# Channel mixers of a two-layer trunk: high and low part of the moving operand in one 512-column product

## The chip, the core and the metric

The kernel runs on one core of a Trainium2 chip. The metric is the device time of one execution in microseconds (us); lower is better. The engines are named as in the profile: PE multiplies matrices (PEld is its weight load), DVE and ACT are the vector and the scalar engine, POOL and SP mostly issue transfers. Results of PE land in PSUM, which the kernel uses as eight banks of 128 x 512 float32; everything else lies in SBUF. In the profile a tile carries the tag of its pool: `pmm`, `psc` and `ptr` are PSUM banks, `u`, `f`, `t`, `pt`, `wr`, `wh`, `wl` are SBUF buffers.

## The reference

The program is an encoder trunk of two layers on 512 tokens of width 1024, float32 in and out. Each layer has a token mixer (matrix memory or band attention, plus attention to 256 memory tokens), an output projection, and a channel mixer. The channel mixer is what the change is about:

```python
def conv_ffn(h, w_up, conv_w, conv_b, w_down):
    u, g = jnp.split(h @ w_up, 2, axis=-1)
    g = causal_dwconv(g, conv_w, conv_b)
    return (jax.nn.silu(g) * u) @ w_down
```

`h` is 512 x 1024 and normalised, the up projection has 2 x 2816 columns (22 tiles of 128 for `u`, 22 for the gate `g`), the convolution has width 3 along the tokens, and the sum of the result and the residual goes on to the next layer.

## The kernel before, in words

**Two parts of every number.** Operands of PE have the type float32r, so each is split into a high part and a low part: `split` (L130 to L133) makes the high part by a cast on ACT (L132) and the low part by a subtraction on DVE (L133). A product of two operands is then three products: high x high (L171), high x low (L172), low x high (L173), all in `mm3`, added up in one PSUM bank.

**Block sums.** In a channel mixer tiles 0 to 4 of the up projection are computed plainly. For tiles 5 to 21 the method `step` computes the tile of `u` and the tile of the gate together as a 2 x 2 block product, with seven chains of products in place of eight. The tokens are two halves of 256 columns (`H`), the 1024 input features two halves of four tiles. The sums of input blocks are made once (`forms`), the sums of weight blocks per step (class `Forms`). The seven chains, in the order in which PE runs them: `a11`, `a12`, `s2`, then a piece of the down projection (`down_products(0)`), `s1`, `s3`, a second piece (`down_products(1)`), `a22`, `s4`. Each chain is four calls of `mm3` with 256 columns, 12 products; a piece of the down projection is 12 products of 512 columns. Steps 9 to 20 have both pieces, steps 5 to 8 only the second, step 21 none (`UNITS`).

**Three banks a step.** `a11`, `s2`, `s3` and `a22` add up in the same bank `r1`, and after each of the four ACT copies the bank's state out (L808, L814, L824, L831): the running sum is itself wanted. `a12` goes to `r2` and is added by DVE (L811). `s1` and `s4` add up in `r3`, read by DVE after each (L825, L907).

**The order is written out.** Inside `later` the orders of PE, ACT and DVE are those of the program text (`manual_schedule`), and each engine takes its list strictly in turn. One pass of `step(j)` also does the rest of tile j-1 (class `Tail`: last block, three taps of the convolution, silu, gating, split) and makes the weights of tile j+1 (class `Forms`: sums and splits). So a step's list on DVE and ACT mixes work for three tiles, and an instruction that waits holds up all that is behind it.

**Around it.** Outside the mixers the order is left to a scheduler. Tiles `u` come from one pool of 57 buffers of 512 columns. Before each mixer `reload_x` brings the residual back from memory in eight transfers of 256 KB that SP issues (L412).

Of the kernel before, what the change touches and what calls it, by code (L numbers as in the profile page):

```python
# [16 lines left out]
P = 128  # L17
D = 1024
S = 512
# [25 lines left out]
UNITS.update((j, (2 * j - 10, 2 * j - 9)) for j in range(9, 21))  # L45
H = S // 2
# [7 lines left out]
def trunk(  # L54
# [25 lines left out]
    bufs = {"wr": 3, "wh": 3, "wl": 3, "u": 57, "t": 8, "pt": 2, "s": 16, "rb": 3, "bias": 2}  # L80
# [4 lines left out]
    def sb(tag, shape, dtype=F32):  # L85
        count[0] += 1
        return pool.tile(shape, dtype, tag=tag, name=f"{tag}{count[0]}", bufs=bufs[tag])

# [207 lines left out]
    def scaled(t, g):  # L296
        hi, lo = sb("u", [P, S], F32R), sb("u", [P, S], F32R)
# [98 lines left out]
    def x_scaled(j):  # L396
# [6 lines left out]
        acts.append((sb("u", [P, S], F32R), sb("u", [P, S], F32R)))  # L403
# [5 lines left out]
    def reload_x():  # L409
        for j in range(KT):  # L410
            xT[j] = sb("u", [P, S])
            tc.keep_in_program_order(nc.sync.dma_start(xT[j], xspill[j]))  # L412
# [6 lines left out]
    with tc.manual_schedule(engines={mybir.EngineType.PE, mybir.EngineType.Activation, mybir.EngineType.DVE}):  # L419
# [9 lines left out]
        for q in range(KT // 2 + 1):  # L429
            if q < KT // 2:  # L430
# [6 lines left out]
                hi, lo = sb("u", [P, S], F32R), sb("u", [P, S], F32R)  # L437
# [3 lines left out]
                kws.append([sb("u", [P, S], F32R).rearrange("p (a b) -> p a b", a=2) for _ in range(2)])  # L441
# [6 lines left out]
        for u in range(4):  # L448
            vws.append([sb("u", [P, S], F32R).rearrange("p (a b) -> p a b", a=2) for _ in range(2)])
# [43 lines left out]
    def head_queries(t, scale=1.0):  # L493
        qs, ls = ([sb("u", [P, S], F32R) for _ in range(2)] for _ in range(2))
# [36 lines left out]
    def values(outs):  # L531
# [5 lines left out]
        hi, lo = sb("u", [P, S], F32R), sb("u", [P, S], F32R)  # L537
# [3 lines left out]
    def queries(o, row):  # L541

        if row is None:
            return head_queries(o, HD**-0.5)
        q = sb("t", [P, S])
        V.scalar_tensor_tensor(q, o, HD**-0.5, row, op0=ALU.mult, op1=ALU.mult)
        return head_queries(q)
# [6 lines left out]
    def memory_attention(q, kv, hp, mixes):  # L554
# [46 lines left out]
        mixes[6 + hp] = values(outs)  # L601
# [34 lines left out]
    class ChannelMixer:  # L636
# [64 lines left out]
        def forms(self):  # L701

            for j in range(KT):
# [3 lines left out]
                hi, lo = sb("u", [P, S], F32R), sb("u", [P, S], F32R)  # L707
# [4 lines left out]
            for k in range(KT // 2):  # L712
# [10 lines left out]
                for t in (ta, tb):  # L723
                    hi, lo = sb("u", [P, S], F32R), sb("u", [P, S], F32R)
                    split(hi, lo, t)
                    pairs.append((hi, lo))
# [49 lines left out]
        def later(self):  # L776
# [17 lines left out]
            for part in (tail.last_block, tail.first_tap, tail.second_tap, tail.third_tap, tail.gated, tail.split):  # L794
                part()

        def step(self, j, w, nxt, tail):
# [4 lines left out]
            new = Tail(self, j)  # L802
# [8 lines left out]
            V.tensor_tensor(out=new.up[:, :H], in0=new.up[:, :H], in1=r2[:, :H], op=ALU.add)  # L811
            then(tail, "third_tap")
            self.products(r1, w.s2, self.t(2))
            A.copy(new.up[:, H:], r1[:, :H])  # L814
# [8 lines left out]
            self.products(r1, w.s3, self.t(3))  # L823
            A.copy(new.u3[:, :H], r1[:, :H])  # L824
# [5 lines left out]
            self.products(r1, w.a22, self.t(4))  # L830
            A.copy(new.pre[:, :H], r1[:, :H])  # L831
            then(nxt, "split_down", "split_gate")
            self.products(new.r3, w.s4, self.b(1, 1))
# [65 lines left out]
    class Tail:  # L899


        def __init__(self, mixer, j):
            self.mixer, self.j = mixer, j

        def last_block(self):
            c = self.up[:, H:]
            V.tensor_tensor(out=c, in0=c, in1=self.r3[:, :H], op=ALU.add)  # L907
# [592 lines left out]
```

## Time and profile before

| | us |
|---|---|
| median of the 3 runs | 1203.18 (1202.53 to 1204.07) |
| the profiled execution | 1203.12 |
| its span | 1201.4 |
| PE busy | 1191.2 (99%) |
| DVE busy | 945.9 (79%) |
| ACT busy | 708.5 (59%) |
| stretch of the first mixer's steps in the span | about 343 to 600 |
| stretch of the second mixer's steps | about 907 to 1165 |

The span is the profiled execution from its first to its last instruction; 1.7 us lie around it. Rows of a timeline give start, duration, engine, line, operation, output and inputs, and in square brackets the idle time of the engine just before and whose end it waited for. Neighbouring instructions of an engine overlap a little, so the distance from one start to the next is shorter than a duration; both are used below, and the text says which.

### The profile page before, as it was taken

What the parts mean: (1) busy time and instruction counts of PE and PEld (TensorE: products, weight loads), DVE (VectorE), ACT (ScalarE), POOL (GpSimd) and SP (SyncE); (2) the same over time, 40 slices, a digit from 0 to 9 for tenths busy, and PEclk for the clock granted to TensorE, in tenths of its full rate; (3) what the DMA queues carried; (4) which work ended last, traced back from release to release, by engine and by line L of the source; (5) the groups of instructions that cost most, each with busy time, mean ns of one, the idle gap of its engine ahead of it and who ended that gap; (6) DMA issues with size and microseconds to landing.
All of it is one profiled execution on the core that took longest, in us unless ns stands there. A gap on an engine that the chain in (4) does not pass through costs nothing.

```text
span 1201.4 us, 18749 instructions
## 1 busy us (share of the span) xinstructions
PE 1191.2 (99%) x7047; PEld 1056.8 (88%) x7047; DVE 945.9 (79%) x1722; ACT 708.5 (59%) x1260; POOL 123.4 (10%) x207
## 2 busy tenths in 40 slices
PE   9999999999999999999999999999999999999997
PEld 8988888888899999999888888888889999999986
DVE  6777687888978777777698888997897877777755
ACT  5546577644556555555565667775465655555545
POOL 2200101010021111111020000001001011011100
PEclk9999999999999999999999999999999999999999
DMA  8634221444275676665563323146336466666551
GB/s 294 203 88 123 54 53 57 152 142 123 79 176 153 154 164 155 156 142 127 141 197 110 90 71 101 51 130 204 112 97 140 111 143 133 142 141 137 120 156 70
DMA packets 199021, 156.00 MB, mean 130 GB/s; under 512 B 7865, under 2 KB 179347, under 8 KB 198931
## 3 DMA queue, kind: packets, MB, share of 16 engines
q1 hardware_dynamic: 183762, 119.73, 34.0%
q0 software_dynamic: 14592, 34.03, 14.4%
q8 instruction: 55, 0.90, 0.3%
q10 hardware_dynamic: 576, 1.05, 0.2%
q14 instruction: 36, 0.29, 0.1%
HBM read 126.27 MB, written 32.44 MB: 132 GB/s over the span
## 4 chain that ended last, share of the span: by engine, by line
PE 93%; ACT 3%; DVE 2%; DMA 0%; issue 0%; SPq 0%; DVEq 0%; ACTq 0%
PE pmm L171 18%; PE pmm L173 18%; PE pmm L172 18%; PE ptr L171 6%; PE ptr L172 6%; PE ptr L173 6%; PE psc L171 5%; PE psc L172 5%; PE psc L173 5%; PE psc L516 2%; PE ptr L1327 1%; PE ptr L1348 1%; PE ptr L1349 1%; DMA u<-in_mem_dram 0%; ACT wh L132 0%
## 5 line engine op out<-in xcount | busy, mean ns | idle before, releaser
L171 PE MATMUL pmm<-u,wh 128*128 128x512 f32 (+1 forms) x968 | 336.6, 348 | 0.1
L173 PE MATMUL pmm<-u,wl 128*128 128x512 f32 (+1 forms) x968 | 333.7, 345 | 0.0
L172 PE MATMUL pmm<-u,wh 128*128 128x512 f32 (+1 forms) x968 | 333.3, 345 | 0.1
L133 DVE TENSOR_TENSOR wl<-wr,wh 128x1024 fp32r<-128x1024 f32 (+3 forms) x172 | 199.7, 1162 | 102.4 <-ACT wh L132 101.8
L132 ACT CAST wh<-wr 128x1024 fp32r<-128x1024 f32 (+3 forms) x172 | 171.8, 1001 | 108.3 <-PE pmm L172 42.8
L173 PEld LDWEIGHTS pmm<-u,wl 128*128 128x128 f32 x968 | 183.6, 190 | 21.1
L172 PEld LDWEIGHTS pmm<-u,wh 128*128 128x128 f32 x968 | 183.8, 190 | 18.3 <-DVE u L133 0.8
L171 PEld LDWEIGHTS pmm<-u,wh 128*128 128x128 f32 x968 | 183.7, 190 | 18.0 <-ACT u L132 0.5
L171 PE MATMUL ptr<-u,wh 128*128 128x512 f32 x272 | 106.7, 392 | 0.0
L172 PE MATMUL ptr<-u,wh 128*128 128x512 f32 x272 | 106.5, 392 | 0.0
L173 PE MATMUL ptr<-u,wl 128*128 128x512 f32 x272 | 105.8, 389 | 0.0
L748 POOL DMA_DIRECT2D xspill<-t x64 | 55.5, 867 | 465.4 <-ACT t L747 454.9
L173 PE MATMUL pmm<-u,u 128*128 128x256 f32 x296 | 84.0, 284 | 0.4 <-DVE u L133 0.4
L171 PE MATMUL pmm<-u,u 128*128 128x256 f32 x296 | 84.0, 284 | 0.0
L172 PE MATMUL pmm<-u,u 128*128 128x256 f32 x296 | 83.7, 283 | 0.0
L133 DVE TENSOR_TENSOR u<-pt,u 128x512 fp32r<-128x512 f32 x102 | 70.2, 688 | 11.7 <-ACT u L132 9.1
L171 PE MATMUL psc<-u,wh 128*128 128x256 f32 (+1 forms) x232 | 76.1, 328 | 0.0
L173 PE MATMUL psc<-u,wl 128*128 128x256 f32 (+1 forms) x232 | 75.9, 327 | 0.0
L172 PE MATMUL psc<-u,wh 128*128 128x256 f32 (+1 forms) x232 | 75.9, 327 | 0.0
L747 ACT COPY t<-ptr 128x512 f32<-128x512 f32 x64 | 37.4, 585 | 60.5 <-PE ptr L173 60.5
L132 ACT CAST u<-pt 128x512 fp32r<-128x512 f32 x102 | 63.0, 617 | 11.3 <-DVE pt L857 11.3
L919 ACT ACTIVATE t<-t 128x512 f32<-128x512 f32 x34 | 21.6, 634 | 79.6 <-DVE t L656 79.6
(291 smaller groups left out, 2527.4 us busy)
## 6 DMA issues: line engine op xcount, KB each, us to landing
wr<-in_ffn_w_up_dram SPq DMA_DIRECT2D x54, 512.0 KB, 4.9
wr<-in_ffn_w_down_dram SPq DMA_DIRECT2D x38, 512.0 KB, 3.9
pt<-in_ffn_w_up_dram SPq DMA_DIRECT2D x34, 512.0 KB, 6.3
xspill<-t POOLq DMA_DIRECT2D x64, 256.0 KB, 4.8
wr<-in_a_w_in_dram SPq DMA_DIRECT2D x20, 512.0 KB, 3.9
xspill<-u POOLq DMA_DIRECT2D x32, 256.0 KB, 2.8
u<-xspill SPq DMA_DIRECT2D x32, 256.0 KB, 5.1
wr<-in_w_kv_dram SPq DMA_DIRECT2D x12, 512.0 KB, 4.0
```

What stands on the lines that cost most here:

```text
L132: high = A.copy(hi, src) if on_act else V.tensor_copy(hi, src)
L133: low = V.tensor_tensor(out=lo, in0=src, in1=f(hi), op=ALU.subtract)
L171: nc.tensor.matmul(o, lh, rh, start=first, stop=False, skip_group_check=more)
L172: nc.tensor.matmul(o, lh, rl, start=False, stop=False, skip_group_check=more)
L173: nc.tensor.matmul(o, ll, rh, start=False, stop=last, skip_group_check=more)
L516: nc.tensor.matmul(o, a, b, start=first and i == 0, stop=i == 1)
L747: A.copy(t, o)
L748: G.dma_start(xspill[j], t, accum_op=ALU.add)
L919: A.activation(self.acc, self.acc, AF.Silu)
L1327: nc.tensor.transpose(tp[:, b * P : (b + 1) * P], es[T, h][:, b * P : (b + 1) * P], ident)
L1348: nc.tensor.matmul(o2[:, s * P :], w, hi_at(pts[h], s, s, TT - s), start=s == 0, stop=False)
L1349: nc.tensor.matmul(o2[:, s * P :], w, lo_at(pts[h], s, s, TT - s), start=False, stop=s == TT - 1)
```

## The change

**Products.** In steps 9 to 20 (`WIDE`) six of the seven chains, all but `s1`, no longer use `mm3`. For each input tile there are two products in place of three: the low part of the weight with the high part of the input (256 columns), and the high part of the weight with both parts of the input at once, 512 columns: the high part's 256 and the low part's 256. The second product fills both halves of the bank, so the bank's right half holds the sum of the products with the low part.

**Additions.** The two halves of the bank have to be added. Where ACT copied the left half, DVE now adds the right half to that copy (`plus`, after `a11`, `s2`, `s3`, `a22`); `a12` gets a second addition on DVE; `s4`'s right half is added by `rest_of_block` in the next step. That is six additions of 128 x 256 a step on DVE.

**Order.** The split of the fourth weight sum (`split_fourth`) moves from the front of the step to behind the copy of `a11`, in all steps from 5 on.

**Buffers.** So that one product can read both parts, they must lie at a fixed distance: tiles' high and low part are now one buffer of 1024 columns (`duo`, tag `f`, 16 of them); the pool `u` has 25 buffers instead of 57. The same memory in all, but in two pools.

**Reload.** In the two token mixers `reload_x` stands later in the text, and POOL issues its eight transfers instead of SP.

```diff
+WIDE = range(9, 21)
-    bufs = {"wr": 3, "wh": 3, "wl": 3, "u": 57, "t": 8, "pt": 2, "s": 16, "rb": 3, "bias": 2}
+    bufs = {"wr": 3, "wh": 3, "wl": 3, "u": 25, "f": 16, "t": 8, "pt": 2, "s": 16, "rb": 3, "bias": 2}
+    def duo():
+        t = sb("f", [P, 2 * S], F32R)
+        return t[:, :S], t[:, S:]
...
-        def products(self, o, w, act, first=False):
+        def products(self, o, w, act, first=False, wide=False):
             n = KT // 2
-            for k in range(n):
-                mm3(o[:, :H], w[0][:, k], w[1][:, k], *act[k], first and k == 0, k == n - 1, True)
+            for k, (hi, lo) in enumerate(act):
+                start, stop = first and k == 0, k == n - 1
+                if wide:
+                    nc.tensor.matmul(o[:, :H], w[1][:, k], hi, start=start, stop=False, skip_group_check=True)
+                    both = bass.AP(
+                        tensor=hi.tensor, offset=hi.offset, ap=[list(hi.ap[0]), [lo.offset - hi.offset, 2], [1, H]]
+                    )
+                    nc.tensor.matmul(
+                        o.rearrange("p (a b) -> p a b", a=2), w[0][:, k], both, start=False, stop=stop,
+                        skip_group_check=True,
+                    )
+                else:
+                    mm3(o[:, :H], w[0][:, k], w[1][:, k], hi, lo, start, stop, True)
...
         def step(self, j, w, nxt, tail):
...
+            wide = j in WIDE
+            def onto_first(w, act, o, first=False):
+                self.products(r1, w, act, first, wide)
+                A.copy(o, r1[:, :H])
+                if wide:
+                    plus(o, r1[:, H:])
+            def plus(o, p):
+                V.tensor_tensor(out=o, in0=o, in1=p, op=ALU.add)
             then(tail, "last_block", "first_tap")
-            w.split_fourth()
             r1, r2, new.r3 = ps("mm"), ps("mm"), ps("sc")
             new.up, new.u3, new.pre = sb("t", [P, S]), sb("t", [P, S]), sb("t", [P, S])
-            self.products(r1, w.a11, self.b(0, 0), True)
-            A.copy(new.up[:, :H], r1[:, :H])
+            onto_first(w.a11, self.b(0, 0), new.up[:, :H], True)
+            then(tail, "rest_of_block")
+            w.split_fourth()
             then(tail, "second_tap")
-            self.products(r2, w.a12, self.b(1, 0), True)
-            V.tensor_tensor(out=new.up[:, :H], in0=new.up[:, :H], in1=r2[:, :H], op=ALU.add)
+            self.products(r2, w.a12, self.b(1, 0), True, wide)
+            plus(new.up[:, :H], r2[:, :H])
+            if wide:
+                plus(new.up[:, :H], r2[:, H:])
             then(tail, "third_tap")
-            self.products(r1, w.s2, self.t(2))
-            A.copy(new.up[:, H:], r1[:, :H])
+            onto_first(w.s2, self.t(2), new.up[:, H:])
...
-            self.products(r1, w.s3, self.t(3))
-            A.copy(new.u3[:, :H], r1[:, :H])
+            onto_first(w.s3, self.t(3), new.u3[:, :H])
...
-            self.products(r1, w.a22, self.t(4))
-            A.copy(new.pre[:, :H], r1[:, :H])
+            onto_first(w.a22, self.t(4), new.pre[:, :H])
             then(nxt, "split_down", "split_gate")
-            self.products(new.r3, w.s4, self.b(1, 1))
+            self.products(new.r3, w.s4, self.b(1, 1), False, wide)
...
-    reload_x()
     fill = chain(outp.part(0, 0, 1), outp.part(0, 2, 6), outp.part(0, 3))
...
     weave(islice(job, 13), fill, 0.85)
+    reload_x(G)
```

**What moves on DVE, front of a step.** DVE's list before, in a late step of the second mixer, from the last block of the tile before (L907) to the second sum of weight blocks (the second L857). `psc` is `r3`, `pmm` is `r2`, L656 are the taps, L133 the low part of the fourth sum.

```order
L907 TENSOR_TENSOR t2276_11722<-t2276_11722,psc2275_11721 128x256
L133 TENSOR_TENSOR u2299_11888<-pt1888_9422,u2298_11887 128x512
L656 SCALAR_TENSOR_TENSOR t2297_11885<-t2278_11724,cols2_793,t2297_11885 128x511
L811 TENSOR_TENSOR t2303_11894<-t2303_11894,pmm2301_11892 128x256
L656 SCALAR_TENSOR_TENSOR t2297_11885<-t2278_11724,cols2_793,t2297_11885 128x510
L857 TENSOR_TENSOR pt1888_9422<-pt1887_9421 128x512
L857 TENSOR_TENSOR pt1888_9422<-pt1888_9422,wr2295_11880 128x512
```

The same piece after the change; L939 is now the last block, L833 is `plus`, L143 the low part, L666 the taps, L889 the sums of weight blocks; `pmm2247` is `r1`, `pmm2248` is `r2`.

```order
L939 TENSOR_TENSOR t2224_11561<-t2224_11561,psc2223_11560 128x256
L833 TENSOR_TENSOR t2250_11713<-t2250_11713,pmm2247_11710 128x256
L939 TENSOR_TENSOR t2224_11561<-t2224_11561,psc2223_11560 128x256
L143 TENSOR_TENSOR u2254_11728<-pt1792_9110,u2253_11727 128x512
L666 SCALAR_TENSOR_TENSOR t2246_11708<-t2226_11563,cols2_769,t2246_11708 128x511
L833 TENSOR_TENSOR t2250_11713<-t2250_11713,pmm2248_11711 128x256 x2
L666 SCALAR_TENSOR_TENSOR t2246_11708<-t2226_11563,cols2_769,t2246_11708 128x510
L833 TENSOR_TENSOR t2250_11713<-t2250_11713,pmm2247_11710 128x256
L889 TENSOR_TENSOR pt1792_9110<-pt1791_9109 128x512
L889 TENSOR_TENSOR pt1792_9110<-pt1792_9110,wr2245_11705 128x512
```

Four instructions came in, and the last of them (`plus` on `s2`) now stands between the third tap and the sums of weight blocks.

**What moves on ACT, front of a step.** ACT's list before: first tap (L663), cast of the fourth sum (L132), copy of `a11` (L808), silu (L919), copy of `s2` (L814).

```order
L663 ACTIVATE t2243_11541<-t2224_11380,cols2_793 128x512
L132 CAST u2244_11543<-pt1888_9422 128x512
L808 COPY t2249_11550<-pmm2246_11547 128x256
L919 ACTIVATE t2243_11541<-t2243_11541 128x512
L814 COPY t2249_11550<-pmm2246_11547 128x256
```

After, with the new line numbers (L828 is every copy of `r1`, L955 the silu):

```order
L673 ACTIVATE t2139_11094<-t2118_10947,cols2_769 128x512
L828 COPY t2143_11099<-pmm2140_11096 128x256
L142 CAST u2146_11113<-pt1792_9110 128x512
L955 ACTIVATE t2139_11094<-t2139_11094 128x512
L828 COPY t2143_11099<-pmm2140_11096 128x256
```

The cast and the copy of `a11` change places; the copy of `s2` still stands behind the silu, which needs the third tap from DVE.

**What moves on DVE, end of a step.** Before, from the low part of the up weights (the first L133, 1024 columns) to the fourth sum:

```order
L133 TENSOR_TENSOR wl2313_11980<-wr2295_11880,wh2312_11979 128x1024
L825 TENSOR_TENSOR t2305_11896<-t2304_11895,psc2302_11893 128x256
L133 TENSOR_TENSOR wl2315_11998<-pt1888_9422,wh2314_11997 128x1024
L857 TENSOR_TENSOR pt1888_9422<-wr2295_11880,pt1888_9422 128x512
L133 TENSOR_TENSOR wl2319_12032<-wr2296_11882,wh2318_12031 128x1024
```

After, in the step whose banks are `pmm2221` (`r1`) and `psc2223` (`r3`):

```order
L143 TENSOR_TENSOR wl2236_11643<-wr2218_11551,wh2235_11642 128x1024
L833 TENSOR_TENSOR t2225_11562<-t2225_11562,pmm2221_11558 128x256
L858 TENSOR_TENSOR t2226_11563<-t2225_11562,psc2223_11560 128x256
L143 TENSOR_TENSOR wl2238_11658<-pt1792_9110,wh2237_11657 128x1024
L889 TENSOR_TENSOR pt1792_9110<-wr2218_11551,pt1792_9110 128x512
L833 TENSOR_TENSOR t2226_11563<-t2226_11563,pmm2221_11558 128x256
L143 TENSOR_TENSOR wl2242_11689<-wr2219_11553,wh2241_11688 128x1024
```

The addition for `s3` (the first L833) stands directly behind the low part of the up weights, and the one for `a22` (the second) between the fourth sum and the low part of the down weights.

More of the change, by code (lines that the diff above doesn't have):

```diff
@@ L448, in trunk @@
         for u in range(4):
-            vws.append([sb("u", [P, S], F32R).rearrange("p (a b) -> p a b", a=2) for _ in range(2)])
+            vws.append([t.rearrange("p (a b) -> p a b", a=2) for t in duo()])
             split(*vws[u], vraw[u])
@@ L489, in trunk, with head_queries @@
         keep(1, 1, vo, A.copy)
-    def head_queries(t, scale=1.0):
-        qs, ls = ([sb("u", [P, S], F32R) for _ in range(2)] for _ in range(2))
+    def head_queries(t, scale=1.0, room=None):
+        qs, ls = ((room or two)() for _ in range(2))
         for h, r in enumerate(HEADS):
@@ L723, in forms @@
                 for t in (ta, tb):
-                    hi, lo = sb("u", [P, S], F32R), sb("u", [P, S], F32R)
-                    split(hi, lo, t)
-                    pairs.append((hi, lo))
+                    pairs.append(duo())
+                    split(*pairs[-1], t)
                 self.sums.append(pairs)
@@ L1117, in a_memory_queries @@
     def a_memory_queries(hp):
-        memq[hp] = queries((yield from project(w_in, 4 * AW + 2 * AH + hp * P, act)), None)
+        memq[hp] = queries((yield from project(w_in, 4 * AW + 2 * AH + hp * P, act)), None, duo if hp else two)
     def mlstm_head(h):
@@ L1350, in band_attention @@
             yield
-        mixes[j] = values(outs)
+        mixes[j] = values(outs, two if j < 5 else duo)
     def b_memory_queries(hp):
-        memq[hp] = queries((yield from project(b_w_in, AW + hp * P, act)), norm.row)
+        memq[hp] = queries((yield from project(b_w_in, AW + hp * P, act)), norm.row, duo if hp else two)
     qkv = {}
```

59 lines of the change are left out of this document (32 added, 27 removed).

## The prediction

> **What bounds the kernel now.** I read the page first, then the busy time by stage, then the timelines of PE, DVE and ACT in one late step of a mixer. The page:
>
> ```profile
> span 1201.4 us, 18749 instructions
> PE 1191.2 (99%) x7047; PEld 1056.8 (88%) x7047; DVE 945.9 (79%) x1722; ACT 708.5 (59%) x1260; POOL 123.4 (10%) x207
> ```
>
> PE has work in 99% of the span, so time can only be won by shortening what PE does, and anything that makes PE wait is paid in full. The stage of the first mixer's steps, by engine:
>
> ```profile
> 340.00:600.00 260.00, 259.90 (x1815) 243.43 (x1814) 193.86 (x284) 145.86 (x249) 41.03 (x55) 1.00 0.64 152
> ```
>
> PE is busy for 259.90 of 260 us at full clock (1.00); DVE, the third figure, for 193.86, which is three quarters. What one product costs there is its distance to the next, in PE's timeline (40 distances in the first pair of rows, 24 in the second):
>
> ```profile
> 899.65 0.39 PE L172 MATMUL ptr<-u,wh 128*128 128x512 f32 x1
> ...
> 908.72 0.39 PE L173 MATMUL ptr<-u,wl 128*128 128x512 f32 x1
> 908.94 0.28 PE L171 MATMUL pmm<-u,wh 128*128 128x256 f32 x1
> ...
> 911.82 0.28 PE L171 MATMUL pmm<-u,u 128*128 128x256 f32 x1
> ```
>
> A product of 512 columns takes 9.07 / 40 = 0.2268 us, one of 256 takes 2.88 / 24 = 0.1200. So two of 256 cost 0.240 and one of 512 costs 0.2268: 0.0133 us are saved for each pair that is merged.
>
> The other two engines, in the step whose last block is added at 1102.11. DVE:
>
> ```profile
> 1102.11 0.41 DVE L907 TENSOR_TENSOR t<-t,psc 128x256 f32<-128x256 f32 x1
> 1102.44 0.69 DVE L133 TENSOR_TENSOR u<-pt,u 128x512 fp32r<-128x512 f32 x1
> 1103.04 0.75 DVE L656 SCALAR_TENSOR_TENSOR t<-t,cols,t 128x511 f32<-128x511 f32 x1
> 1103.71 0.42 DVE L811 TENSOR_TENSOR t<-t,pmm 128x256 f32<-128x256 f32 x1
> 1104.04 0.75 DVE L656 SCALAR_TENSOR_TENSOR t<-t,cols,t 128x510 f32<-128x510 f32 x1
> 1104.70 0.69 DVE L857 TENSOR_TENSOR pt<-pt 128x512 f32<-128x512 f32 x1
> 1105.42 0.69 DVE L857 TENSOR_TENSOR pt<-pt,wr 128x512 f32<-128x512 f32 x1
> ...
> 1108.66 0.69 DVE L133 TENSOR_TENSOR u<-t,u 128x512 fp32r<-128x512 f32 x1 [0.56 <-ACT u L132]
> 1109.61 1.23 DVE L133 TENSOR_TENSOR wl<-wr,wh 128x1024 fp32r<-128x1024 f32 x1 [0.26 <-ACT wh L132]
> ...
> 1115.93 1.23 DVE L133 TENSOR_TENSOR wl<-wr,wh 128x1024 fp32r<-128x1024 f32 x1 [2.35 <-ACT wh L132]
> 1117.07 0.69 DVE L133 TENSOR_TENSOR u<-pt,u 128x512 fp32r<-128x512 f32 x1
> 1117.67 0.41 DVE L907 TENSOR_TENSOR t<-t,psc 128x256 f32<-128x256 f32 x1
> ```
>
> and ACT:
>
> ```profile
> 1104.88 0.63 ACT L919 ACTIVATE t<-t 128x512 f32<-128x512 f32 x1 [2.53 <-DVE t L656]
> 1105.41 0.36 ACT L814 COPY t<-pmm 128x256 f32<-128x256 f32 x1
> 1106.15 0.62 ACT L132 CAST u<-pt 128x512 fp32r<-128x512 f32 x1 [0.38 <-DVE pt L857]
> 1107.52 0.59 ACT L747 COPY t<-ptr 128x512 f32<-128x512 f32 x1 [0.75 <-PE ptr L173]
> 1108.01 0.62 ACT L132 CAST u<-t 128x512 fp32r<-128x512 f32 x1
> 1108.53 1.05 ACT L132 CAST wh<-wr 128x1024 fp32r<-128x1024 f32 x1
> ...
> 1114.58 0.37 ACT L831 COPY t<-pmm 128x256 f32<-128x256 f32 x1 [0.85 <-PE pmm L173]
> 1114.85 1.05 ACT L132 CAST wh<-wr 128x1024 fp32r<-128x1024 f32 x1
> ```
>
> From L907 to the next L907 a step takes 15.56 us, which is PE's own: 7 chains x 12 x 0.120 and 24 products of 0.2268 are 15.52. The brackets are where DVE and ACT ran ahead and waited; DVE had 0.56 + 0.26 + 2.35 us to spare.
>
> **The products.** A step of the wide kind has 6 chains x 4 = 24 merged pairs, so PE's own time falls by 24 x 0.0133 = 0.32, to 15.24. With 12 such steps in two mixers that is 576 pairs and 7.7 us, the whole of what the change can win. No row before shows a product that reads its 512 columns as two runs of 256. Bounds: 0.2268 as one run, 0.240 if it behaved as two; I take 0.2268, since the runs are long and no row speaks against it.
>
> The Trainium skill ("TensorE: Matmul & The Clock Gate", Back-to-back issue gap) puts a product at its columns over 2.4 GHz plus 2.5 ns, so a merged pair would save only 2.5 ns, 1.4 us in all. The rows above show 13.3 ns, and they decide; by the page's figure PE's own step would be 15.50 and my total 0.5 higher.
>
> **The additions.** Six a step, each of the form of L811 (one operand in PSUM): 0.33 from start to start (1103.71 to 1104.04), 2.0 in all. That fits into DVE's 3.2 to spare. What matters is where they stand, since DVE and ACT take their lists in turn, and the bank `r1` may not be written before its copy and, now, its addition are done. I walked the new order with the distances above. The place that decides is the third tap: DVE's next instruction is now the addition for `s2`. It waits for ACT's copy of `s2`, which stands behind the silu, which waits for that very tap. Before, DVE went on with the sums of weight blocks. All that follows on DVE comes later by this wait, down to the addition for `s3`, and `a22` on PE waits for that one. What such a wait costs PE is seen once before, in step 21:
>
> ```profile
> 590.33 0.37 ACT L824 COPY t<-pmm 128x256 f32<-128x256 f32 x1
> 590.75 0.19 PEld L171 LDWEIGHTS pmm<-u,u 128*128 128x128 f32 x1 [0.35 <-ACT t L824]
> 590.98 0.28 PE L172 MATMUL pmm<-u,u 128*128 128x256 f32 x1
> ```
>
> The copy ends at 590.70, the load starts 0.05 later, and the second product comes at 590.98 instead of 0.12 after the load: 0.16 from the end of the copy to a product on time.
>
> So there is a closed circle, and its length is the shortest step that DVE, ACT and PE together allow. From the addition for `s3`: addition and release of PE 0.42 + 0.16; `a22` 4 x (0.120 + 0.227) less one distance, plus the last product's 0.39, 1.55, and 0.04 to ACT; copy to the low part of the down weights 1.35 (1114.58 to 1115.93); that low part 1.14, the gate's 0.60, last block 0.33; addition for `a11` 0.33, rest of the block 0.33; the fourth's low part 0.60; second tap 0.67; first addition for `a12` 0.42 + 0.03 (the second needs its result, as 1104.70 to 1105.42 is 0.72 for 0.69), the second 0.33; third tap 0.75 and 0.09 to the silu; silu 0.53; copy 0.37 + 0.03; addition for `s2` 0.33; first sum 0.72; second 0.73 to ACT's cast (1105.42 to 1106.15); cast 0.52, copy of the down piece 0.49, cast of the tile's result 0.52; cast of the up weights 1.05 + 0.03; its low part 1.14. The sum is 15.59.
>
> 15.59 is above PE's 15.24, and even above today's 15.56. So the win of a wide step is used up: `a22` waits 0.35 in each. Only step 9, which has no wide step before it, keeps its 0.32. Steps 10 to 20 are 11 x 0.03 = 0.33 longer in each mixer.
>
> **The moved split.** In steps 6, 7, 8 and 21, which stay narrow, the cast of the fourth sum now stands behind the copy of `a11`, and DVE's list waits for it. From the start of `a11`: its result at 1.60, copy 1.64, cast 1.91, low part from 2.56, second tap 3.16, addition 3.83, third tap 4.16, silu 5.00, copy of `s2` 5.53, release of PE 5.53 + 0.37 + 0.16 = 6.06. PE is through with `a11`, `a12`, `s2` and `s1` at 4 x 1.44 = 5.76. `s3` waits 0.30, 4 times a mixer: 1.2.
>
> **Buffers and reload.** In the token mixers PE is as full, so these can only cost. The two pools hold as many columns as one held, and the tiles of `duo` are freed together. I price both at nothing, with 1.5 us either way for a scheduler's other order. The reload moves off SP to POOL, behind the last mask of the last head:
>
> ```profile
> xspill<-t POOLq DMA_DIRECT2D x64, 256.0 KB, 4.8
> 237.59 0.64 POOL L1135 TENSOR_SCALAR_AFFINE_SELECT t<-t 128x128 f32<-128x128 f32 x1 [0.52 <-ACT t L1133]
> ...
> 257.38 0.69 DVE L629 TENSOR_TENSOR u<-u,pmm 128x512 f32<-128x512 f32 x1 [1.02 <-PE pmm L173]
> ```
>
> Between the end of that mask and the first use lie 19 us, and such a transfer takes 4.8 to land: hidden.
>
> **Sum.** Per mixer -0.32 + 0.33 + 1.2 = 1.2, for two 2.4. On the profiled execution's 1203.12 (0.06 from the median) that is 1205.5.
>
> **Rivals.** (1) *The cover holds*: the circle is shorter than 15.24 and PE runs through. For it speaks DVE's idle share; against it that 0.35 would have to be wrong in a sum whose terms are rows of the same step. Then 1203.1 - 7.7 + 2.4 = 1197.8. This is the other side, and it decides at a circle of 15.24.
> (2) *Dearer waits*: the silu's release took 0.09 where others took 0.03. If the three new ones in the circle (copy to addition, addition to addition, addition to PE) each cost 0.06 more, it is 15.77, 22 x 0.18 = 4.0 more: 1209.5.
> (3) *Late reload*: if POOL's eight transfers land 2 us after the first use in both layers, 1209.5; the 19 us speak against it.
> (4) *The change doesn't do what it says*: a product in two runs takes 0.240. PE's own time stays, `a22` in the circle is 0.05 longer, so 1.1 more: 1206.6.
>
> The Trainium skill ("Perfetto Trace Analysis", Optimizing Tensor Performance, Matmuls) advises both larger products and a change of banks between chains, so that reading one out overlaps the next. This change takes the first and makes the second worse. In the trace before, the reuse of `r1` stopped PE in step 21 (0.35, above); by the first advice alone it would be rival 1.
>
> **Chances.** The forecast 0.63, rival 1 0.11, rival 2 0.16, rivals 3 and 4 0.05 each. A measurement of this kernel can tell about 0.2%, 2.4 us, from no change, and the forecast lies on that bound. Of its 0.63 I put 0.22 above 1205.6, 0.38 within, and 0.03 below 1200.8. With the rivals: faster 0.14, same 0.40 (0.02 from rival 4), slower 0.46. The range: down, 0.1 of error in the circle is 2.2, and 1.5 for the order elsewhere, with something over for rival 1; up, rival 2 with half a microsecond over: 1199.5 to 1210. Rival 1 itself is left out.
>
> **What would show it.** Right: products of 512 columns at 0.227 in the mixers; a wait of about 0.35 a step on PE before `a22`, on DVE; about 1 us of idle DVE before the addition for `s2`, on ACT's copy; steps of 15.6 us; 0.3 before `s3` in steps 6 to 8. Wrong: steps of 15.24 with no such waits (rival 1), steps over 15.7, or PE idle for microseconds outside the mixers.

## The result and the profile after

| | before | after |
|---|---|---|
| median us (runs) | 1203.62 (4 runs, 1202.53 to 1205.06) | 1211.99 (4 runs, 1211.44 to 1212.88) |
| span of the profiled execution, us | 1201.4 | 1211.1 |
| wide step of a mixer (10 to 20), us | 15.56 | 15.60 to 15.62 |

Steps 9 to 20, where the change merges products, are called wide here, the others (5 to 8 and 21) narrow. The changed kernel is slower by 0.7%: 1.0069 of the time before, with a 95% interval of 1.0057 to 1.0081, or 8.4 us. The forecast was 1205.5, its range ended at 1210.0. The page of the kernel after:

```profile
span 1211.1 us, 17719 instructions
PE 1196.9 (99%) x6471; PEld 1024.7 (85%) x6471; DVE 995.5 (82%) x1866; ACT 707.3 (58%) x1260; POOL 131.5 (11%) x223
```

576 products are gone, and yet PE is busy for 5.7 us more: part of what it waits is counted as busy (the row at 489.48 below is a product of 256 columns that takes 0.39). So the page's busy time says nothing here; what tells is where PE falls behind. For that each product of the profile after was set beside the same product of the profile before; the lag is how much later it starts. It grows by these amounts, and by nothing in the stretches not listed:

| stage (us of before) | lag grows by |
|---|---|
| start, 0 to 31 | 0.9 |
| first token mixer, 31 to 319 | 0.3 |
| plain tiles before the first mixer, 319 to 334 | 1.3 |
| first mixer, 349 to 612 | 1.5 |
| 612 to 778 | -0.5 |
| second token mixer, 778 to 838 | 3.0 |
| plain tiles before the second mixer, 884 to 899 | 1.4 |
| second mixer, 914 to 1161 | 1.7 |

The 0.9 at the start is a tile that landed later in this one execution (mixers as before, copy before silu and fourth split in front, which have the same start, lag by 0.1 at most). The two mixers lose 3.2. Three short stretches outside them lose 5.7, and of these the prediction said that they cost nothing.

**The mixers.** The stretch from 340 to 600 by engine, and what PE's weight loads wait for in it (total, times, longest):

```profile
340.00:600.00 260.00, 259.82 (x1523) 226.71 (x1522) 219.28 (x356) 145.07 (x249) 41.69 (x56) 1.00 0.67 148
```

```profile
PEld pmm L777 <- DVE t L833: 4.5, 11, 0.5
PEld pmm L181 <- ACT t L828: 1.3, 5, 0.3
```

DVE went from 193.86 to 219.28 us, still 84%: it is not the bound by its sum. L833 is the new addition, L828 the copy ahead of it. There are eleven waits for the addition, one in each wide step from 10 on, 0.41 each; of the five for the copy, four are those of the narrow steps, 0.23 each, and one stood before too. DVE and ACT around the addition for `s2` and the one for `s3` show why:

```profile
481.71 0.74 DVE L666 SCALAR_TENSOR_TENSOR t<-t,cols,t 128x510 f32<-128x510 f32 x1
483.48 0.42 DVE L833 TENSOR_TENSOR t<-t,pmm 128x256 f32<-128x256 f32 x1 [1.02 <-ACT t L828]
...
489.01 0.41 DVE L833 TENSOR_TENSOR t<-t,pmm 128x256 f32<-128x256 f32 x1
...
504.62 0.41 DVE L833 TENSOR_TENSOR t<-t,pmm 128x256 f32<-128x256 f32 x1
```

```profile
482.55 0.63 ACT L955 ACTIVATE t<-t 128x512 f32<-128x512 f32 x1 [3.31 <-DVE t L666]
483.09 0.35 ACT L828 COPY t<-pmm 128x256 f32<-128x256 f32 x1
```

The third tap ends at 482.45, the silu (L955) starts at 482.55, the copy of `s2` behind it at 483.09, and DVE stands 1.02 us idle until the copy is there. At 489.01 the addition for `s3` starts, and 15.61 later the next one; PE's `a22` needs its bank:

```profile
489.10 0.39 PE L183 MATMUL ptr<-u,wl 128*128 128x512 f32 x1
489.48 0.39 PE L777 MATMUL pmm<-f,u 128*128 128x256 f32 x1
489.70 0.39 PE L781 MATMUL pmm<-f,u 128*128 128x512 f32 x1
489.93 0.28 PE L777 MATMUL pmm<-f,u 128*128 128x256 f32 x1
490.05 0.40 PE L781 MATMUL pmm<-f,u 128*128 128x512 f32 x1
```

The first product of `a22` comes 0.38 after the last one ahead of it, where 0.23 is usual, and the second 0.22 after the first, where 0.12 is: PE loses 0.25. The rows also show the new product's price: 0.23 from a product of 512 columns (L781) to the next. Over all of them in the mixers the mean is 0.233, not 0.2268.

**Outside the mixers.** PE's weight loads in the plain tile at 324 (three rows):

```profile
323.80 0.19 PEld L182 LDWEIGHTS pmm<-f,wh 128*128 128x128 f32 x1
324.95 0.19 PEld L183 LDWEIGHTS pmm<-f,wl 128*128 128x128 f32 x1 [0.96 <-DVE wl L143]
325.06 0.19 PEld L181 LDWEIGHTS pmm<-f,wh 128*128 128x128 f32 x1
```

PE waits 0.96 for the low part of the weights. These rows lead up to it: on DVE the low part of earlier weights and, at 323.68, the one that PE needs; SP's load of the raw weights (`wr`) for it; ACT's cast of the high part:

```profile
317.19 1.21 DVE L143 TENSOR_TENSOR wl<-wr,wh 128x1024 fp32r<-128x1024 f32 x1
...
323.68 1.22 DVE L143 TENSOR_TENSOR wl<-wr,wh 128x1024 fp32r<-128x1024 f32 x1
```

```profile
318.47 0.37 SPq L155 DMA_DIRECT2D wr<-in_ffn_w_up_dram  x1
```

```profile
322.59 1.05 ACT L142 CAST wh<-wr 128x1024 fp32r<-128x1024 f32 x1 [0.30 <-DMA wr<-in_ffn_w_up_dram]
```

and the same two low parts and the same load before:

```profile
314.21 1.22 DVE L133 TENSOR_TENSOR wl<-wr,wh 128x1024 fp32r<-128x1024 f32 x1
...
320.50 1.22 DVE L133 TENSOR_TENSOR wl<-wr,wh 128x1024 fp32r<-128x1024 f32 x1 [0.29 <-ACT wh L132]
```

```profile
315.49 0.37 SPq L145 DMA_DIRECT2D wr<-in_ffn_w_up_dram  x1
```

PE is 1.18 behind at this place; the low part is 3.18 behind. DVE has no idle time ahead of it. But it could not have made it sooner: ACT's cast ends at 323.64, and the cast waits for the load. The load is 2.98 late, because there are three buffers `wr`, and in both kernels it is issued 0.06 to 0.07 after a low part of earlier weights is done (at 318.40, and at 315.43 before). Two low parts further back the lateness is larger still: 306.12 against 300.13. There DVE's list has 15 instructions between this low part and the one before it, and had 9. So the order of DVE's list makes the low parts late, and the lateness comes down to PE through the loads.

### The profile page after: what moved, and what is told of

It reads as the page before. It is cut to its first block, busy times and chain, and to the rows that moved or that the text cites. A ratio compares the mean times of both kernels' runs of the same rounds, so it can differ in the third digit from the quotient of the medians.

```text
span 1211.1 us, 17719 instructions
## 1 busy us (share of the span) xinstructions
PE 1196.9 (99%) x6471; PEld 1024.7 (85%) x6471; DVE 995.5 (82%) x1866; ACT 707.3 (58%) x1260; POOL 131.5 (11%) x223
## 4 chain that ended last, share of the span: by engine, by line
PE 93%; ACT 3%; DVE 2%; DMA 2%; issue 1%; SPq 0%; DVEq 0%; ACTq 0%
PE pmm L181 13%; PE pmm L182 13%; PE pmm L183 13%; PE pmm L781 9%; PE ptr L181 6%; PE ptr L182 6%; PE ptr L183 6%; PE pmm L777 5%; PE psc L183 4%; PE psc L181 4%; PE psc L182 4%; PE psc L526 2%; PE psc L781 2%; PE ptr L1363 1%; PE psc L777 1%; DMA wr<-in_ffn_w_up_dram 1%
## 5 line engine op out<-in xcount | busy, mean ns | idle before, releaser
L143 DVE TENSOR_TENSOR wl<-wr,wh 128x1024 fp32r<-128x1024 f32 (+3 forms) x172 | 199.6, 1161 | 58.9 <-ACT wh L142 56.7
L181 PE MATMUL pmm<-f,wh 128*128 128x512 f32 (+1 forms) x584 | 218.2, 375 | 0.5 <-ACT t L828 0.3
L183 PE MATMUL pmm<-f,wl 128*128 128x512 f32 (+1 forms) x584 | 215.3, 369 | 1.1 <-DVE wl L143 1.1
L182 PE MATMUL pmm<-f,wh 128*128 128x512 f32 (+1 forms) x584 | 214.3, 367 | 0.7 <-DVE f L143 0.6
L183 PEld LDWEIGHTS pmm<-f,wl 128*128 128x128 f32 x584 | 110.2, 189 | 19.3 <-DVE wl L143 1.9
L181 PEld LDWEIGHTS pmm<-f,wh 128*128 128x128 f32 x584 | 110.2, 189 | 16.9 <-ACT t L828 2.2
L182 PEld LDWEIGHTS pmm<-f,wh 128*128 128x128 f32 x584 | 110.4, 189 | 16.2 <-DVE f L143 2.0
L781 PE MATMUL pmm<-f,wh 128*128 128x512 f32 x288 | 103.1, 395 | 0.0
L143 DVE TENSOR_TENSOR u<-pt,u 128x512 fp32r<-128x512 f32 x102 | 70.2, 688 | 18.9 <-ACT u L142 16.2
L833 DVE TENSOR_TENSOR t<-t,pmm 128x256 f32<-128x256 f32 x154 | 64.1, 416 | 25.5 <-ACT t L828 24.4
L828 ACT COPY t<-pmm 128x256 f32<-128x256 f32 x136 | 50.1, 368 | 53.8 <-PE pmm L781 29.5
L777 PE MATMUL pmm<-f,wl 128*128 128x256 f32 x288 | 80.9, 281 | 0.0
L955 ACT ACTIVATE t<-t 128x512 f32<-128x512 f32 x34 | 21.5, 633 | 99.2 <-DVE t L666 99.2
L183 PE MATMUL psc<-f,wl 128*128 128x256 f32 (+1 forms) x220 | 71.3, 324 | 0.0
L182 PE MATMUL psc<-f,wh 128*128 128x256 f32 (+1 forms) x220 | 71.2, 324 | 0.0
L181 PE MATMUL psc<-f,wh 128*128 128x256 f32 (+1 forms) x220 | 71.1, 323 | 0.0
```

What stands on the lines that cost most here:

```text
L143: low = V.tensor_tensor(out=lo, in0=src, in1=f(hi), op=ALU.subtract)
L181: nc.tensor.matmul(o, lh, rh, start=first, stop=False, skip_group_check=more)
L182: nc.tensor.matmul(o, lh, rl, start=False, stop=False, skip_group_check=more)
L183: nc.tensor.matmul(o, ll, rh, start=False, stop=last, skip_group_check=more)
L777: nc.tensor.matmul(o[:, :H], w[1][:, k], hi, start=start, stop=False, skip_group_check=True)
L781: nc.tensor.matmul(o.rearrange("p (a b) -> p a b", a=2), w[0][:, k], both, start=False, stop=stop, skip_group_check=True,)
```

## The experiments

Twelve kernels, each timed in five rounds against the kernel before (5 to 11 runs). The medians of before lay between 1203.2 and 1203.6 each time.

| kernel | median us | ratio to before, 95% interval |
|---|---|---|
| mixers as before (pools and reload only) | 1209.01 | 1.0045, 1.0032 to 1.0058 |
| reload alone | 1203.62 | 0.9998, 0.9989 to 1.0007 |
| pools alone | 1208.28 | 1.0042, 1.0029 to 1.0056 |
| copy before silu | 1203.92 | 1.0005, 0.9997 to 1.0014 |
| fourth split in front | 1209.48 | 1.0053, 1.0041 to 1.0066 |
| sums woven | 1204.30 | 1.0009, 1.0001 to 1.0018 |
| all woven | 1204.87 | 1.0012, 1.0004 to 1.0021 |
| weights first | 1205.93 | 1.0023, 1.0014 to 1.0032 |
| low products first | 1202.42 | 0.9993, 0.9984 to 1.0002 |
| queries double | 1203.21 | 1.0001, 0.9992 to 1.0010 |
| all together | 1197.01 | 0.9948, 0.9936 to 0.9961 |
| all together, sums woven | 1197.59 | 0.9951, 0.9937 to 0.9964 |

**Inside or outside the mixers?** Three kernels take the change apart. The first leaves the mixers as they were:

```
-WIDE = range(9, 21)
+WIDE = ()
...
             then(tail, "last_block", "first_tap")
+            w.split_fourth()
...
             then(tail, "rest_of_block")
-            w.split_fourth()
```

> The changed kernel with the channel mixers as they were: no wide products, the split of the fourth sum back in front of a11. What is left of the change are the two buffer pools and the reload on POOL. My theory now: the mixers cost about 3 us of the 8.4, the rest (5 to 6) comes from outside them, so 1208.5 to 1209.5. Rival A (the mixers and their additions cost everything, the gaps outside are chance): 1203.6 within 1. Rival B (the mixers would have gained and the outside costs more than the whole): above 1212. In the trace: PE gaps on DVE's and ACT's splits in the plain tiles before each mixer, 1.5 us behind before at each, and 3 us more in the second token mixer.

Measured: 1209.01, so 5.6 of the 8.4 us are outside the mixers, and 3.0 are theirs. Rivals A and B fall.

The second is the kernel before with only the reload moved:

```
-            tc.keep_in_program_order(nc.sync.dma_start(xT[j], xspill[j]))
+            tc.keep_in_program_order(queue.dma_start(xT[j], xspill[j]))
...
     weave(islice(job, 13), fill, 0.85)
+    reload_x(G)
```

(and the same in the second token mixer, with the two old calls taken out).

> The kernel before with one edit: the reload of x goes to POOL, at the later place of the changed kernel; pools, mixers and the order of PE, DVE and ACT stay as before. My theory (the reload is hidden as I predicted, the pools cost): 1203.6 within 1. Rival (the reload makes the outside cost): 1206.5 to 1209.5, with PE or DVE waiting for u from POOL's queue at the first additions of the output projection.

Measured: 1203.62, 0.9998 of before. The reload is hidden.

The third has only the pools: the first kernel with the reload on SP at its old place.

```
     run(fill)
+    reload_x()
...
-    reload_x(G)
```

> The kernel before with one edit: 57 buffers become 25 single and 16 double ones, the pairs that the change makes double are double; the reload stays on SP at its old place and the mixers as before. My theory (pools alone): 1208.5 to 1209.5, the same as with the reload on POOL. Rival (the reload): 1203.6 within 1. If both share: 1205 to 1207.

Measured: 1208.28. The pools alone cost 4.9 us. The 0.7 between this kernel and the first lies within both intervals.

**The circle.** One step of it is undone: ACT copies `s2` before it takes the silu.

```
             then(tail, "third_tap")
             onto_first(w.s2, self.t(2), new.up[:, H:])
+            then(tail, "silu")
...
         def third_tap(self):
             next(self.taps)
+
+        def silu(self):
             A.activation(self.acc, self.acc, AF.Silu)
```

> The changed kernel with one edit: on ACT the copy of s2 stands ahead of the silu of the previous tile, so DVE's addition for s2 no longer waits for silu. My theory (a closed circle through the silu, 15.59 a step): the circle opens, wide steps fall to PE's own 15.23, the narrow steps 6 to 8 and 21 lose their 0.30 too, 5.1 less in each mixer: 1202 (1201 to 1203). Rival (the additions load DVE as such, or the wide products do not save): wide steps stay at 15.5 to 15.6, 1210 to 1212.

Measured: 1203.92, 8.1 less than the changed kernel. What PE's loads wait for from 340 to 600 now, and DVE and ACT at the place of the 1.02 us:

```profile
PEld pmm L181 <- ACT u L142: 0.5, 1, 0.5
PEld pmm L181 <- ACT t L828: 0.3, 1, 0.3
PEld pmm L182 <- DVE u L143: 0.2, 1, 0.2
```

```profile
479.28 0.74 DVE L666 SCALAR_TENSOR_TENSOR t<-t,cols,t 128x510 f32<-128x510 f32 x1
479.94 0.41 DVE L833 TENSOR_TENSOR t<-t,pmm 128x256 f32<-128x256 f32 x1
```

```profile
478.80 0.37 ACT L828 COPY t<-pmm 128x256 f32<-128x256 f32 x1 [1.93 <-PE pmm L781]
480.12 0.63 ACT L958 ACTIVATE t<-t 128x512 f32<-128x512 f32 x1 [0.95 <-DVE t L666]
```

The eleven waits for the addition are gone, and so are those of the narrow steps; the one for the copy that is left stood before too. The copy is there at 479.17, before the third tap ends, and DVE doesn't wait. So the circle through the silu is shown. But the wide steps fall to 15.38, not to the 15.23 expected: without any wait, PE's own step is 0.15 longer. That is the product, and the reason why the time lies above the 1201 to 1203 expected.

**The narrow steps.** The moved split goes back in front of `a11` where a step is narrow:

```
             then(tail, "last_block", "first_tap")
+            if not wide:
+                w.split_fourth()
...
             then(tail, "rest_of_block")
-            w.split_fourth()
+            if wide:
+                w.split_fourth()
```

> The changed kernel with one edit: where a step is narrow (5 to 8 and 21) the split of the fourth sum stands in front of a11 again. My theory: the waits of 0.30 before s3 go in steps 6, 7, 8 and 21 of both mixers, 2.4 less: 1209.6. Rival (those waits only move to a later place in the step, or are the scheduler's chance): 1212. Wide steps stay at 15.60.

Measured: 1209.48, 2.5 less than the changed kernel. The eight waits cost what was worked out for them.

**The wide product.** By turns with one of 256 columns it takes 0.236 to the next, as the kernel with the copy before silu shows at `s3`:

```profile
489.87 0.40 PE L781 MATMUL pmm<-f,wh 128*128 128x512 f32 x1
490.11 0.28 PE L777 MATMUL pmm<-f,wl 128*128 128x256 f32 x1
490.22 0.40 PE L781 MATMUL pmm<-f,wh 128*128 128x512 f32 x1
```

A pair takes 0.35, where three products of 256 took 0.36. The first idea was that it reads two runs of 256. Two kernels weave the tiles, so that it reads one run of 512; first those of the sums, then those of the input too:

```
+    def woven():
+        t = sb("f", [P, 2 * S], F32R).rearrange("p (h a b) -> p h a b", h=2, a=2)
+        return t[:, :, 0, :], t[:, :, 1, :]
...
-                    pairs.append(duo())
-                    split(*pairs[-1], t)
+                    pairs.append(woven())
+                    split(*pairs[-1], t.rearrange("p (h b) -> p h b", h=2))
```

> The kernel of the last experiment (copy before silu, 1203.9), with one edit: the tiles of the sums of the input hold high and low parts of each half side by side, so that the wide products of s2, s3 and a22 read one run of 512 columns; those of a11, a12 and s4 still read two runs of 256. In the last experiment a wide product took 0.236 to the next, an ordinary one of 512 columns 0.227. Theory (the two runs cost the 0.009): 0.227 for the wide products on the sums and 0.236 for the others, 12 x 0.009 less in each of 24 steps, 2.6: 1201.3. Rival (the 0.009 comes from the change of width between neighbours, 256 and 512, or from the bank): 0.236 for all, 1203.9.

> As the kernel with woven sums, and the tiles of the input itself woven as well: all wide products read one run, and in exchange the 192 products of 512 columns that use these tiles in the plain tiles 3 and 4 read two. Theory (two runs cost 0.009): wide products 0.227 everywhere, 5.2 less than 1203.9, the plain ones 0.236 and 1.7 more: 1200.4. Rival (not the runs): 1203.9, and the plain ones stay at 0.227.

Measured: 1204.30 and 1204.87, no faster than 1203.92. The second kernel's products of one run, where L786 is the wide one:

```profile
483.14 0.40 PE L786 MATMUL pmm<-f,wh 128*128 128x512 f32 x1
483.38 0.28 PE L782 MATMUL pmm<-f,wl 128*128 128x256 f32 x1
483.50 0.40 PE L786 MATMUL pmm<-f,wh 128*128 128x512 f32 x1
```

0.24 and 0.12 again. The mean is 0.236 with one run and with two. The plain products are the clean half of this test, since all their neighbours have 512 columns. Those that now read two runs:

```profile
322.20 0.39 PE L186 MATMUL psc<-f,wh 128*128 128x512 f32 x1
322.43 0.39 PE L187 MATMUL psc<-f,wh 128*128 128x512 f32 x1
322.65 0.39 PE L188 MATMUL psc<-f,wl 128*128 128x512 f32 x1
```

They stay at 0.227 (the median of 188). My theory falls.

Then the order: the four products of 256 columns first, the four wide ones behind them.

```
+            for k, (hi, lo) in enumerate(act if wide else ()):
+                nc.tensor.matmul(o[:, :H], w[1][:, k], hi, start=first and k == 0, stop=False, skip_group_check=True)
             for k, (hi, lo) in enumerate(act):
                 start, stop = first and k == 0, k == n - 1
                 if wide:
-                    nc.tensor.matmul(o[:, :H], w[1][:, k], hi, start=start, stop=False, skip_group_check=True)
```

> The kernel with the copy before silu (1203.9) with one edit: in a wide chain the four products with the weights' low parts (256 columns) come first, then the four of 512 columns, instead of one after the other by turns. By turns a pair took 0.117 + 0.236 = 0.353, where 0.120 and 0.227 were expected (0.347). Theory (the change of width between neighbours costs 6 ns a pair): 0.347 a pair again, 24 x 0.006 less in each of 24 steps, 3.5 in all: 1200.4. Rival (a product of 512 columns that adds into a bank half of which was begun by one of 256 costs this, in any order): 1203.9.

Measured: 1202.42, 1.5 less than 1203.92, less than half of what the theory wanted. The chain of `s3`, four products in a row each (L775 those of 256, L782 the wide ones):

```profile
489.15 0.64 PE L775 MATMUL pmm<-f,wl 128*128 128x256 f32 x4
489.63 1.09 PE L782 MATMUL pmm<-f,wh 128*128 128x512 f32 x4
490.56 0.63 PE L775 MATMUL pmm<-f,wl 128*128 128x256 f32 x4
```

0.48 and 0.93: a wide one takes 0.233 here, and wide steps 15.30. A pair takes 0.351, against 0.353 by turns and the 0.347 expected: a smaller part of the surcharge is due to the turns, the larger is not.

**The plain tiles.** On the kernel with pools and reload only, the splits of the plain tiles' weights get a higher priority; no buffer changes.

```
-        wh, wl = weights(rows(w, c0, P), n, P)
+        raw = load(rows(w, c0, P), n, P)
+        with tc.high_priority(ahead) if ahead else ExitStack():
+            wh, wl = parts(raw)
...
-            gate = project(self.w, DFF + j * P, act)
-            up = project(self.w, j * P, act, "sc")
+            gate = project(self.w, DFF + j * P, act, ahead=100)
+            up = project(self.w, j * P, act, "sc", 100)
```

> The kernel with the two pools and the reload on POOL and the mixers as before (1209.0), with one edit: the splits of the weights of the plain tiles are given a higher priority in the scheduler, 100 places. Nothing in the buffers changes. My theory (the pools cost by the other order of DVE's and ACT's lists, in which the plain tiles' weights come late, 1.4 before each mixer): those waits go, 1206.2, and the 2 us in the second token mixer stay. Rival (the pools cost because buffers run out, whatever the order): 1209.0 within 0.7. If the new order is worse elsewhere it is above.

Measured: 1205.93, 3.1 less than 1209.01. Set beside that kernel, PE gains 1.3 in the plain tiles before the first mixer and 1.4 before the second, and nothing between; no wait of PE's loads is left from 300 to 340. The low part for which PE waited (made at 323.68 in the changed kernel, at 320.50 before):

```profile
314.88 1.23 DVE L143 TENSOR_TENSOR wl<-wr,wh 128x1024 fp32r<-128x1024 f32 x1 [0.67 <-ACT wh L142]
```

It is ready 8.8 earlier, as the low parts ahead of it come earlier and with them the loads. The kernel before has no wait of PE's loads from 300 to 345 or from 880 to 915, so the priority wins nothing here but what the pools cost. These waits came from the order of the lists alone.

**The second token mixer.** POOL zeroes the unused halves of queries. The four of the last heads before, and the same four after:

```profile
757.43 2.37 POOL L496 MEMSET u<- 64x512 f32 x4 [23.43 <-PE pmm L173]
```

```profile
759.24 1.09 POOL L506 MEMSET f<- 64x512 f32 x2 [21.48 <-PE pmm L183]
782.97 1.09 POOL L506 MEMSET u<- 64x512 f32 x2 [22.64 <-PE psc L526]
```

Two of them are taken from the single buffers, and wait until PE's scores (L526) give one back: 24 us later. Here it is a buffer that is missing. What this costs PE can be read in the kernel with the weights first. ACT fills these queries (`u`) at 780.30, where it filled them at 773.43 before; it comes to the memory's queries (`f`) only behind them, and PE waits for those:

```profile
780.30 1.28 ACT L509 ACTIVATE u<-t 64x512 fp32r<-64x512 f32 x2
...
782.90 1.28 ACT L509 ACTIVATE f<-t 64x512 fp32r<-64x512 f32 x2
```

```profile
784.88 0.54 PEld L528 LDWEIGHTS psc<-u,f 128*128 128x128 f32 x4 [0.69 <-ACT f L512]
```

Another 1.1 PE waits later on, for DVE's part of the last pair's softmax (L1350). With the weights first as well, the last pair's queries are now taken from the double buffers:

```
-        q = queries((yield from project(b_w_in, j * P, act)), norm.row)
+        q = queries((yield from project(b_w_in, j * P, act)), norm.row, duo if j == 5 else two)
```

> The kernel with pools, reload, mixers as before and the weights' splits first (1205.9), with one edit: the queries of the second token mixer's last pair of heads (pair 5) are taken from the double buffers, which are free there, and no longer from the 25 single ones. In the traces POOL zeroes these queries at 757 before, at 780 with the two pools, where it waits for PE's scores to release a single buffer. Theory (the single buffers run out there, and that makes the 2 us of the second token mixer): 1203.9. Rival (the 2 us come from the order of the lists, as in front of the mixers): 1205.9 within 0.7.

Measured: 1203.21, the same as before (1.0001), and below the 1203.9 expected. All four are zeroed at 755 to 759, so double ones did stand free:

```profile
755.65 1.08 POOL L508 MEMSET f<- 64x512 f32 x2 [21.50 <-PE pmm L183]
757.66 1.19 POOL L508 MEMSET f<- 64x512 f32 x2 [0.93 <-PE pmm L183]
```

ACT fills the last pair's queries at 773.68 again, and neither of the two waits is left. So the whole cost outside the mixers is found: 3.1 by order, 2.7 by single buffers, against 5.6 measured. The medians carry some tenths; by the lag in the traces it is 2.7 and 2.4.

**All together.**

> The changed kernel with all edits that bore or should bear something: the copy of s2 before silu, low products first in a wide chain, the plain tiles' weights first, the queries of pair 5 in double buffers. If the parts add up: 1203.9 - 3.5 - 3.1 - 2.0 = 1195.3, faster than both kernels. If the low products first bring nothing: 1198.8. Rival (the parts don't add up: with PE shorter than 15.3 a step the next circle through DVE and ACT stops it): 1199 to 1201, with waits of PE in the mixers.

Measured: 1197.01, 0.9948 of before (0.9936 to 0.9961). From the changed kernel's 1211.99 the four edits take 8.1, 1.5, 3.1 and 2.7 one by one; that leaves 1196.6, so they add up; the 1195.3 expected had counted the order of the products at 3.5. What is won against before, 6.2, is 24 wide steps of 0.26 (15.56 to 15.30); by the lag PE gains 3.1 in each mixer. In the mixers PE's loads wait no longer than this for an addition (from 340 to 600; the other waits there are single ones):

```profile
PEld pmm L777 <- DVE t L836: 1.7, 11, 0.2
```

and these 0.16 lie beside products that still run: steps have the same 15.30 as in the kernel with low products first.

The last kernel weaves the sums once more, now that wide products stand in a row:

> The kernel with all edits together (1197.0) with one more: the tiles of the sums are woven, so that the wide products of s2, s3 and a22 read one run of 512 columns, those of a11, a12 and s4 two runs. With the low products first, a wide product took 0.233 to the next wide one, where ordinary ones of 512 columns take 0.227; by turns with the low ones the number of runs made no difference, which may have been hidden by the turns. Theory (a second run costs 0.006 where wide products stand in a row): 0.227 on the sums, 0.233 on the others, 12 x 0.006 less in 24 steps, 1.7: 1195.3. Rival (it is not the reading): 0.233 for both, 1197.0 within 0.7.

Measured: 1197.59; 0.232 with one run, 0.234 with two. But without the weaving these same chains take 0.232 and 0.234 too, so it is not the reading.

## Why the prediction was right or wrong

- **The product** (0.2268 as one run): mis-sized. It took 0.233 in the changed kernel and 0.236 where nothing waits. PE's own wide step is 15.38, not 15.24, so the most that the change could win in this form was 24 x 0.18 = 4.3, not 7.7. Of the price that I called the other bound, 0.240, two thirds came true, but not for the reason given there and in rival 4, since one run costs the same. In this kernel it decided nothing, because the circle was longer than either. The Trainium skill ("TensorE: Matmul & The Clock Gate", Back-to-back issue gap) puts the gap of a single product at its columns over 2.4 GHz plus 2.5 ns; an estimate from this figure has a merged pair save 2.5 ns. The step shows 0.18 / 24 = 7.5 ns, so the trace agrees with neither it nor my 13.3.
- **The additions and the circle**: right, and not by luck. 15.59 was worked out (the terms as listed add up to 15.60), 15.60 to 15.62 measured, and the single terms hold: from the addition for `s3` to the copy of `a22` 2.17 was worked out and 2.17 measured (489.01 to 491.18), from there to the low part of the down weights 1.35 and 1.35 (to 492.53). DVE idle 1.02 before the addition for `s2` (about 1), `a22` waiting in each wide step from 10 on. Its cost to PE is 0.25 rather than 0.35, as PE's own step is longer by what the product costs more. Step 9 kept 0.12 of its win (by so much the lag falls there), not 0.32. Rival 1 falls with this, and rival 2 too: the new waits are not dearer than the old (from the end of the addition, 489.42, to PE's second product 0.28, and from the end of the copy in step 21 before 0.28 as well). The Trainium skill ("Perfetto Trace Analysis", Optimizing Tensor Performance, Matmuls) advises larger products and a change of banks between independent chains. The first is borne out, 15.38 a step for 15.56. On the second the trace shows what the reuse of `r1` costs, eleven waits of 0.41 in a mixer; no run here gave the chains other banks.
- **The moved split**: right, 2.4 worked out, 2.5 measured.
- **The reload**: right, hidden; rival 3 falls.
- **The buffers**: this is the step that failed. "The two pools hold as many columns as one held, and the tiles of `duo` are freed together. I price both at nothing, with 1.5 us either way for a scheduler's other order." They cost 4.9 alone and 5.6 with the reload. That the columns are as many is true and doesn't help: a double buffer can't serve a single tile, and in the second token mixer the 25 single ones ran out while double ones were free. And the other order was not worth 1.5 either way: it alone cost about 3. In the plain tiles before a mixer DVE has little to spare (in the kernel before it is busy for 18.77 of 19 us from 300 to 319, for 13.85 of 15 from 319 to 334 and for 14.08 of 15 from 884 to 899, against three quarters in the steps), so a list that puts the weights' low parts later was paid by PE. Why the scheduler's order changed just so was not taken apart; that the order made the cost is shown.
- **The sum**: 2.4 for the mixers, where 3.0 was measured; nothing for the rest, where 5.6 was. The prediction named what would refute it, "PE idle for microseconds outside the mixers", and that is what happened: PE falls behind by 5.7 in three short stretches there.

## What to carry to other kernels

Where one engine is busy all the time, an added instruction on an engine with time to spare is priced by the place it takes in that engine's list: walk the closed circles through the engines, and move what stands in the longest one (here one copy, 8.1 us). Splitting a pool of buffers is an edit of the schedule in every stage that uses it; go through the stages where another engine is nearly full or where buffers are waited for, and price each. A change that loses may still hold a gain: repaired at four places, this one is 0.5% faster than before.

## What was not expected of the hardware

A product of 512 columns that adds into the same bank as products of 256 takes 0.236 to the next where the two alternate, and 0.233 where four follow each other, against 0.227 for ordinary ones of the same size in the same steps. Reading one run or two made no difference: 0.236 and 0.236 by turns; in a row 0.232 and 0.234, which the same chains show unwoven too; and plain products that read two runs stay at 0.227. Nor is it a bank of which only one half has been begun: with the copy before silu, `s3` and `a22`, whose bank already holds sums in both halves, take 0.236 and 0.235, and `a11` and `a12`, which begin theirs, 0.236 and 0.237. What makes the surcharge stays open. The neighbours' width is the smaller part at most, as four in a row still take 0.233; traffic of other engines was not taken apart.
